# The state products of the decode streams as pairs in two halves of the array's rows, one pair behind each half of the output projection

## The chip, the cores and the metric

The kernel runs on one core of one Trainium2 chip. The metric is device time in microseconds (us) of one execution. The core has a matrix engine (TensorE; PE in the profile, PEld for its weight loads), a vector engine (VectorE, DVE), a scalar engine (ScalarE, ACT), a general engine (GpSimd, POOL) and a queue that issues most DMAs (SyncE, SP). All engines run side by side and wait for each other by semaphores; each one carries out its own instructions in order.

## The reference

One inference step of a two-layer trunk, on 1024 prompt frames and on 8 running streams of 16 frames each. Layer 0 is a gated MLP. Layer 1 is an mLSTM block with 4 heads of width 512; the change lies in it. For each head `h` and each running stream `b` the layer keeps a 512x512 matrix memory `C`:

```python
num   = einsum('bhts,bhse->bhte', s, v) + w_inter[..., None] * einsum('bhtd,bhde->bhte', q, C)
C_new = decay[..., None, None] * C + einsum('bhs,bhsd,bhse->bhde', w, k, v)
out   = (h + skip * xc) * silu(z);   y = x + out @ w_out
```

So for each of the 32 pairs of head and stream the 1 MB of old memory (`C0`) is read, multiplied by 16 query rows (the inter term of `num`), decayed, added to a product of 16 keys and 16 values, and written out (`C_sample`).

## The kernel before

Everything is single precision. A product that must be exact to about 24 bits is split in a high and a low part, and three matmuls are added up (high by high, high by low, low by high), each at the speed of one pass (type F32R).

**Streams.** Each pair of head and stream is one `Stream` (L1119). `load` (L1124) requests `sk48` (48 rows: the 16 keys and 16 values in the three combinations of high and low part, from the scratch tensor `st_d`) and the old memory as two tiles `c0` of 128x2x512 (256 of its 512 rows each). `products` (L1132) does two things. First the query product: 4 matmuls, one for each 128 rows of the memory, each using 32 of the array's 128 columns, so that the four lie side by side (`sm<-c,qT` in the profile; each is two instructions, so 8 rows of the trace). Its result is copied by ScalarE (`ev`, L1141). Then the state products: 4 matmuls of 48 rows by 128x512 (`sm<-sk`), each into a PSUM tile of its own; VectorE decays and adds each one into `c0` (L1148) and each half of `c0` is stored (L1150). Every fourth stream `finish` (L1152) gathers the query products (`sm<-ev,selm`).

**When streams run.** 10 of the 32 streams run inside the projection of `z` (a dense row of matmuls `sm<-xh,w` and `sm<-xl,w`, L867 to L879), placed by the table `plan` (L1433 to L1446). The other 22 run in the loop over units, one in each of the units 0 to 21 (L1490). The pools hold one `sk48` and four `c0` tiles (two streams).

**Units.** A unit is one 128-frame chunk of one head; there are 4 x 8. Unit n = 0 of a head is short, since it has no earlier state and no state update. In the order of TensorE, a unit does its own numerators (`sm<-va,s`, `sm<-Ch,q`), the state update (`sm<-va,k`), the scores of the next unit (`sm<-qT,kT`, `sm<-ident,kT`), the output projection of the unit two before (`project(prev2, 0)` and `(prev2, 1)`: 12 matmuls `sm<-w,o` each, for the two halves of the 1024 output columns; each half is added to `x1` by VectorE, L1399), the transposes of the unit before (`gate_pe`, `sm<-ident,hn`), and then the stream of this unit. The gate of the unit before follows those transposes: VectorE (`raw`, L1380), then GpSimd or, for chunks 0 to 2, VectorE (L1382), then ScalarE and GpSimd split the result into `o2` (`o<-raw`, L89 and L90), which the output projection of the next unit reads.

**What sets the order.** TensorE's order is the program's order. On the other engines a scheduler places each instruction by its own estimate of when its inputs are ready; there each engine is bound to the order that was written. PSUM has 8 tiles, all named `sm`, in rotation.

Of the kernel before, what the change touches and what calls it, by code (L numbers as in the profile page):

```python
# [8 lines left out]
F32 = mybir.dt.float32  # L9
F32R = mybir.dt.float32r  # L10
# [5 lines left out]
P = 128  # L16
# [54 lines left out]
def trunk_kernel(ctx: ExitStack, tc: tile.TileContext, ins: dict, outs: list):  # L71
# [12 lines left out]
    def f32(ap):  # L84
        return ap.bitcast(F32)
# [371 lines left out]
    def part(ks, q):  # L457
        return Xh[:, ks, quarter(q)], Xl[:, ks, quarter(q)]
# [660 lines left out]
    class Stream:  # L1119
# [2 lines left out]
            self.c0 = [None, None]  # L1122

        def load(self):  # L1124
            d, b = self.d, self.b
            self.sk = dw.tile([3 * SL, 2, DH], F32R, name="sk48")
            S.dma_start(out=f32(self.sk), in_=f32(st_d[d.h])[b])
            for hf in range(2):
                c0 = self.c0[hf] = dw.tile([P, 2, DH], F32, name="c0", bufs=4)
                S.dma_start(out=c0, in_=C0[b, d.h, hf * 256:(hf + 1) * 256].rearrange("(c p) e -> p c e", p=P))  # L1130

        def products(self):  # L1132
            d, b = self.d, self.b
            pa = ps.tile([P, DH], F32, name="sm")

            b2 = slice(b // 2 * 32, b // 2 * 32 + 32)
            for c in range(DC):
                T.matmul(pa[32 * c:32 * c + 32], d.g["qT"][:, c, b2], self.c0[c // 2][:, c % 2], start=True, stop=True)
            ev = dw.tile([P, DH], F32, name="ev", bufs=4)
            d.ev.append(ev)  # L1140
            d.last = A.copy(out=ev, in_=pa)  # L1141
            for hf in range(2):
                c0 = self.c0[hf]
                for cc in range(2):
                    c = hf * 2 + cc
                    pc = ps.tile([P, DH], F32, name="sm")
                    T.matmul(pc, self.sk[:, 0, c * P:(c + 1) * P], self.sk[:, 1, :], start=True, stop=True)
                    V.scalar_tensor_tensor(out=c0[:, cc], in0=c0[:, cc], scalar=decB[:, d.h, 8 + b:9 + b], in1=pc,  # L1148
                                           op0=ALU.mult, op1=ALU.add)
                S.dma_start(out=C_s[0, b, d.h, hf * 256:(hf + 1) * 256].rearrange("(c p) e -> p c e", p=P), in_=c0)  # L1150
# [16 lines left out]
    def open_head():  # L1167
        heads.append(Dec(len(heads), streams[-1].d.last if streams else None))

    def open_stream():  # L1170
        st = Stream(heads[len(streams) // SB], len(streams) % SB)
        streams.append(st)
        st.load()


    ld = ctx.enter_context(tc.tile_pool(name="ld", bufs=2, reuse_waits="tile"))
# [260 lines left out]
    for j in range(ZDEC):  # L1437
        k = first + int(j * rate)
        plan.setdefault(k, []).append(open_stream)
        plan.setdefault(k + 2, []).insert(0, lambda j=j: streams[j].products())  # L1440
        plan.setdefault(k + 3, []).insert(0, lambda j=j: streams[j].finish())
        if j % SB == SB - 3 and k + 3 <= 3 * NF:
            plan.setdefault(k, []).append(open_head)
            plan.setdefault(k + 1, []).append(lambda: heads[-1].queries())
            plan.setdefault(k + 2, []).append(lambda: heads[-1].keys())
            plan.setdefault(k + 3, []).append(lambda: heads[-1].normaliser())  # L1446
# [2 lines left out]

    def open_streams(i):  # L1450
        for _ in range(stream_at.count(i)):
            open_stream()
        return streams[len(streams) - stream_at.count(i):]

    def first_loads():
# [34 lines left out]
    for i, u in enumerate(units):  # L1490
# [44 lines left out]
                S.dma_start(out=x1[v.n], in_=x1_d[v.n])  # L1535
        if i + 1 < NU:
            project(prev2, 0)
            project(prev2, 1)
        gate_pe(prev)
        gate(prev)  # L1540
        gate2(prev)
# [7 lines left out]
        if rid3:  # L1549
            project(rid3, 0)  # L1550
            project(rid3, 1)
        for st in sts:
            st.products()
        next_streams = open_streams(i + 1)
        if rid2:
            gate_pe(rid2)
            gate(rid2)
# [49 lines left out]
```

## Time and profile before

| | |
|---|---|
| time, 3 runs | 1933.91 us median (1932.88 to 1936.3) |
| the profiled execution | 1929.5 us, span of its instructions 1927.8 us |
| granted TensorE clock | 0.996 of 2.4 GHz |
| TensorE busy | 1887.7 us (98%) |
| VectorE, ScalarE, GpSimd busy | 63%, 45%, 35% |
| DMA | 328.20 MB, 170 GB/s over the span |

The z projection with its 10 streams lies between about 1200 and 1385 us, the loop of units from there to the end. Busy times of TensorE are modelled ends; the distance from the start of one group to the start of the next is the safer measure.

### The profile page before, as it was taken

Reading aid. Unit: us, or ns where it says so; the run is one execution under the profiler, and the core shown is the slowest. Engines: PE = TensorE matmul, PEld = TensorE weight load, DVE = VectorE, ACT = ScalarE, POOL = GpSimd, SP = SyncE. Lnnn points to the kernel's source line nnn. Section 1 sums busy time; section 2 is a strip of 40 time slices with the busy share of each in tenths; the row PEclk is TensorE's granted clock in tenths of the full one; section 3 lists DMA queues with packets and bytes.
Section 4 is the critical chain, followed back from the end, with each engine's and each line's share of the span. In section 5 each row is a group of like instructions: output and inputs, shape, how many; then the busy total and the mean of one; then the engine's idle time right before and its main releaser. Section 6 shows DMA issues by size and latency. Waiting matters only on the chain.

```text
span 1927.8 us, 32016 instructions
## 1 busy us (share of the span) xinstructions
PE 1887.7 (98%) x11553; PEld 1676.0 (87%) x11553; DVE 1216.1 (63%) x2406; ACT 862.4 (45%) x1760; POOL 674.9 (35%) x725
## 2 busy tenths in 40 slices
PE   7999999999999999999999999999999999999998
PEld 6888999999999778888999989888977887788887
DVE  5832567777776454567666655222388687688786
ACT  5422444444444343446655554222354444444564
POOL 2000234444442000024444421100167457457586
PEclk9999999999999999999999999999999999999999
DMA  6222343333334854435555564787898898876543
GB/s 217 93 93 73 96 109 100 100 98 99 101 97 122 263 152 143 131 92 157 152 160 166 164 186 124 240 256 247 263 320 267 263 287 273 262 239 196 153 130 125
DMA packets 345305, 328.20 MB, mean 170 GB/s; under 512 B 28164, under 2 KB 276436, under 8 KB 345148
## 3 DMA queue, kind: packets, MB, share of 16 engines
q1 hardware_dynamic: 278444, 255.72, 43.4%
q10 hardware_dynamic: 66512, 69.85, 11.7%
q8 instruction: 91, 1.49, 0.3%
q14 instruction: 66, 0.54, 0.1%
q0 software_dynamic: 192, 0.59, 0.1%
HBM read 203.07 MB, written 123.02 MB: 169 GB/s over the span
## 4 chain that ended last, share of the span: by engine, by line
PE 79%; DMA 7%; DVE 5%; POOL 3%; ACT 2%; issue 2%; ACTq 0%; SPq 0%; POOLq 0%; DVEq 0%
PE sm L58 79%; DMA cw<-cw_d 1%; POOL Cl L90 1%; DMA out<-c 1%; DMA z_d<-st 1%; DVE c L1148 1%; POOL va L90 1%; DMA kT<-k_d 1%; DMA vv<-vb_d 1%; DMA c<-in_state_mlstm_C 1%; DVE raw L1380 0%; DVE w L90 0%; DMA st_d<-w 0%; POOL q L90 0%; DVE Cst L1297 0%
## 5 line engine op out<-in xcount | busy, mean ns | idle before, releaser
L58 PE MATMUL sm<-xh,w 128*128 128x384 f32 x1536 | 410.4, 341 | 1.8 <-issue 1.2
L58 PEld LDWEIGHTS sm<-xh,w 128*128 128x128 f32 x1536 | 281.0, 188 | 10.0 <-issue 6.5
L58 PE MATMUL sm<-xl,w 128*128 128x384 f32 x768 | 260.1, 339 | 0.0
L58 PE MATMUL sm<-Xh,w 128*128 128x288 f32 x1024 | 216.9, 299 | 4.3 <-ACT c L499 4.3
L58 PE MATMUL sm<-w,o 128*128 128x512 f32 x864 | 209.7, 398 | 2.1 <-ACT o L89 1.2
L58 PE MATMUL sm<-w,os 128*128 128x512 f32 x864 | 200.3, 393 | 4.5 <-ACT os L89 3.5
L58 PEld LDWEIGHTS sm<-w,os 128*128 128x128 f32 x864 | 162.4, 189 | 40.8 <-ACT os L89 6.0
L58 PEld LDWEIGHTS sm<-w,o 128*128 128x128 f32 x864 | 160.0, 188 | 40.2 <-ACT o L89 1.4
L58 PE MATMUL sm<-w,Xh 128*128 128x512 f32 x576 | 180.5, 394 | 0.9 <-DVE w L90 0.9
L58 PEld LDWEIGHTS sm<-Xh,w 128*128 128x128 f32 x1024 | 168.9, 190 | 4.7 <-ACT c L499 4.5
L58 PE MATMUL sm<-S,w 128*128 128x288 f32 x1152 | 163.8, 297 | 0.0
L90 DVE TENSOR_TENSOR w<-r,w 128x512 fp32r<-128x512 f32 x176 | 137.9, 790 | 35.1 <-ACT w L89 34.4
L58 PEld LDWEIGHTS sm<-S,w 128*128 128x128 f32 x1152 | 155.1, 188 | 0.8
L90 POOL TENSOR_TENSOR Cl<-Cst,Ch 128x514 fp32r<-128x514 f32 x96 | 128.7, 1352 | 73.6 <-ACT Ch L89 50.3
L58 PE MATMUL sm<-Xl,w 128*128 128x288 f32 x512 | 151.9, 297 | 0.0
L58 PEld LDWEIGHTS sm<-xl,w 128*128 128x128 f32 x768 | 144.8, 189 | 0.0
L90 DVE TENSOR_TENSOR w<-raw,w 128x1024 fp32r<-128x1024 f32 x43 | 55.9, 1300 | 130.6 <-ACT w L89 126.6
L89 ACT CAST w<-r 128x512 fp32r<-128x512 f32 x176 | 107.2, 618 | 61.5 <-PE sm L58 29.1
L58 PEld LDWEIGHTS sm<-w,Xh 128*128 128x128 f32 x576 | 108.2, 190 | 24.0 <-DVE w L90 1.8
L58 PE MATMUL sm<-w,Xl 128*128 128x512 f32 x288 | 113.0, 392 | 0.0
L90 DVE TENSOR_TENSOR os<-or,os 128x384 fp32r<-128x384 f32 x96 | 52.8, 555 | 88.0 <-ACT os L89 87.8
L58 PE MATMUL sm<-va,k 128*128 128x258 f32 (+1 forms) x768 | 102.9, 284 | 0.5 <-DVE raw L1380 0.4
(310 smaller groups left out, 3643.5 us busy)
## 6 DMA issues: line engine op xcount, KB each, us to landing
c<-in_state_mlstm_C SPq DMA_DIRECT2D x64, 512.0 KB
out<-c SPq DMA_DIRECT2D x64, 512.0 KB
r<-in_a_w_in SPq DMA_DIRECT2D x96, 256.0 KB
or<-o_d SPq DMA_DIRECT2D x96, 192.0 KB
raw<-in_b_w_in SPq DMA_DIRECT2D x32, 512.0 KB
qT<-q_d SPq DMA_DIRECT2D x40, 256.0 KB
vh<-v_d SPq DMA_DIRECT2D x48, 192.0 KB
vb_d<-st ACTq DMA_DIRECT2D x48, 192.0 KB
```

Source lines behind the costliest of these rows:

```text
L58: ins = fn(*args, **kw)
L89: first = A.copy(out=hi, in_=src)
L90: (lo_eng or V).tensor_tensor(out=lo, in0=src, in1=f32(hi), op=ALU.subtract)
L1148: V.scalar_tensor_tensor(out=c0[:, cc], in0=c0[:, cc], scalar=decB[:, d.h, 8 + b:9 + b], in1=pc, op0=ALU.mult, op1=ALU.add)
```

## The change

The 4 state products of a stream become 2 pairs. `sk48` is held twice, on partitions 0 to 47 and 64 to 111 (two requests instead of one, so 192 KB more for each stream), and the two matmuls of a pair take one copy each, so that they use different halves of the array's rows. `products` now ends after the first pair (`part(0)`); the second is `part(1)`. In the units the query product and the first pair stand between the two halves of the output projection, the second pair behind the second half, and the transposes of the unit before come after that. The `C0` of the next stream is requested between the pairs, its `sk48` behind the second pair. Inside the z projection both pairs stand together, where the four matmuls stood.

```diff
         def load(self):
+            self.load_c0()
+            self.load_sk()
+
+        def load_sk(self):
             d, b = self.d, self.b
-            self.sk = dw.tile([3 * SL, 2, DH], F32R, name="sk48")
-            S.dma_start(out=f32(self.sk), in_=f32(st_d[d.h])[b])
+
+            self.sk = dw.tile([64 + 3 * SL, 2, DH], F32R, name="sk48")
+            for r0 in (0, 64):
+                S.dma_start(out=f32(self.sk)[r0:r0 + 3 * SL], in_=f32(st_d[d.h])[b])
+
+        def load_c0(self):
...
             d.last = A.copy(out=ev, in_=pa)
-            for hf in range(2):
+            self.part(0)
+
+        def part(self, hf):
...
                 c0 = self.c0[hf]
-                for cc in range(2):
+                pcs = [ps.tile([P, DH], F32, name="sm") for _ in range(2)]
+                for cc, pc in enumerate(pcs):
                     c = hf * 2 + cc
-                    pc = ps.tile([P, DH], F32, name="sm")
-                    T.matmul(pc, self.sk[:, 0, c * P:(c + 1) * P], self.sk[:, 1, :], start=True, stop=True)
+                    rs = slice(64 * cc, 64 * cc + 3 * SL)
+                    T.matmul(pc, self.sk[rs, 0, c * P:(c + 1) * P], self.sk[rs, 1, :], start=True, stop=True)
+                for cc, pc in enumerate(pcs):
                     V.scalar_tensor_tensor(out=c0[:, cc], in0=c0[:, cc], scalar=decB[:, d.h, 8 + b:9 + b], in1=pc,
                                            op0=ALU.mult, op1=ALU.add)
...
-        plan.setdefault(k + 2, []).insert(0, lambda j=j: streams[j].products())
+        plan.setdefault(k + 2, []).insert(0, lambda j=j: (streams[j].products(), streams[j].part(1)))
...
         if i + 1 < NU:
             project(prev2, 0)
+        for st in sts:
+            st.products()
+        next_streams = open_streams(i + 1)
+        if i + 1 < NU:
             project(prev2, 1)
+        for st in sts:
+            st.part(1)
+        for st in next_streams:
+            st.load_sk()
         gate_pe(prev)
         gate(prev)
         gate2(prev)
...
-        for st in sts:
-            st.products()
-        next_streams = open_streams(i + 1)
```

On TensorE, at the end of unit 8, the first unit of head 1, before (`w,o` is the output projection, `c` and `sk` the stream's two kinds of product, `ident,hn` the transposes for the gate):

```order
L58 MATMUL sm<-w,o_15667 128x512 x24
L58 MATMUL sm<-ident,hn 128x128 x4
L58 MATMUL sm<-c_15693,qT 32x512 x2
L58 MATMUL sm<-c_15695,qT 32x512 x2
L58 MATMUL sm<-sk_15691 128x512 x4
L58 MATMUL sm<-va_12485,s_15745 128x258 x3
```

and the same place now:

```order
L58 MATMUL sm<-w,o_15713 128x512 x12
L58 MATMUL sm<-c_15674,qT 32x512 x2
L58 MATMUL sm<-c_15676,qT 32x512 x2
L58 MATMUL sm<-sk_15699 128x512 x2
L58 MATMUL sm<-w,o_15713 128x512 x12
L58 MATMUL sm<-sk_15699 128x512 x2
L58 MATMUL sm<-ident,hn 128x128 x4
L58 MATMUL sm<-va_12485,s_15764 128x258 x3
```

The stream's products moved ahead of the transposes, and these now stand directly before the next unit's numerators.

On VectorE, from the end of unit 7 into unit 8, before (`x1` is the addition of a projected half, `raw` the gate's four instructions, `c0` the four state additions, `dd` the masking of the scores that were computed in unit 8):

```order
L1399 TENSOR_TENSOR x1_5_14031<-x1_5_14031,sm_15628 128x512
L1399 TENSOR_TENSOR x1_5_14031<-x1_5_14031,sm_15642 128x512
L1380 SCALAR_TENSOR_TENSOR raw_15661<-sm_15656,colB_235,sk_15492 128x128 x4
L1148 SCALAR_TENSOR_TENSOR c0_15488<-c0_15488,decB_12439,sm_15677 128x512
L1148 SCALAR_TENSOR_TENSOR c0_15488<-c0_15488,decB_12439,sm_15680 128x512
L1148 SCALAR_TENSOR_TENSOR c0_15490<-c0_15490,decB_12439,sm_15684 128x512
L1148 SCALAR_TENSOR_TENSOR c0_15490<-c0_15490,decB_12439,sm_15687 128x512
```

and now:

```order
L1415 TENSOR_TENSOR x1_5_14042<-x1_5_14042,sm_15646 128x512
L1164 SCALAR_TENSOR_TENSOR c0_15440<-c0_15440,decB_12439,sm_15667 128x512
L1164 SCALAR_TENSOR_TENSOR c0_15440<-c0_15440,decB_12439,sm_15668 128x512
L1415 TENSOR_TENSOR x1_5_14042<-x1_5_14042,sm_15678 128x512
L1164 SCALAR_TENSOR_TENSOR c0_15442<-c0_15442,decB_12439,sm_15692 128x512
L1164 SCALAR_TENSOR_TENSOR c0_15442<-c0_15442,decB_12439,sm_15693 128x512
L1396 SCALAR_TENSOR_TENSOR raw_15707<-sm_15702,colB_235,sk_15510 128x128 x4
```

Two state additions moved ahead of the second projected half, and the gate stands behind all four instead of ahead of them.

On ScalarE in unit 8, before (`o` is the high part of the gated rows that the next output projection reads, `s` the high part of the masked scores):

```order
L1329 COPY hn<-sm 128x256
L89 CAST o_15667<-raw 128x512
L1241 ACTIVATE k_15741<-sm,tok 128x512
L89 CAST s_15745<-dd 128x128
L89 CAST q_15750<-dd 128x128
```

and now:

```order
L1345 COPY hn<-sm 128x256
L1257 ACTIVATE k_15760<-sm,tok 128x512
L89 CAST s_15764<-dd 128x128
L89 CAST o_15713<-raw 128x512
L89 CAST q_15769<-dd 128x128
```

The split of `o` moved behind that of `s`. It is the same in unit 16.

## Rows read from the trace of the kernel before

**Rows 1.** The page: TensorE's busy share, and the chain that ended last.
```profile
PE 1887.7 (98%) x11553; PEld 1676.0 (87%) x11553; DVE 1216.1 (63%) x2406; ACT 862.4 (45%) x1760; POOL 674.9 (35%) x725
...
PE 79%; DMA 7%; DVE 5%; POOL 3%; ACT 2%; issue 2%; ACTq 0%; SPq 0%; POOLq 0%; DVEq 0%
```

**Rows 2.** Busy time by stage, 1372 to 1780 us.
```profile
1372.00:1780.00 408.00, 402.36 (x2654) 329.31 (x2653) 315.17 (x679) 186.56 (x368) 235.67 (x213) 1.00 0.85 264
```

**Rows 3.** Groups by shape from 1200 us: busy us, mean ns, idle before.
```profile
L58 PE MATMUL sm<-sk 48*128 48x512 f32 x128 | 39.3, 422 | 4.2 <-DVE x L1399 3.4 <-DMA sk<-st_d 0.8
...
L58 PE MATMUL sm<-c,qT 128*32 128x512 f32 x256 | 34.1, 605 | 0.0
```

**Rows 4.** Timeline at a stream, loads too: start, us, xcount.
```profile
1498.61 0.16 PEld L58 LDWEIGHTS sm<-c,qT 128*32 128x32 f32 x8 [0.37 <-issue]
1498.62 1.06 PE L58 MATMUL sm<-c,qT 128*32 128x512 f32 x8
```

**Rows 5.** Timeline, TensorE, a stream inside the z projection.
```profile
1251.23 1.06 PE L58 MATMUL sm<-c,qT 128*32 128x512 f32 x8
1252.23 1.19 PE L58 MATMUL sm<-sk 48*128 48x512 f32 x4
1253.35 0.45 PE L58 MATMUL sm<-xh,w 128*128 128x384 f32 x1
```

**Rows 6.** Timeline, TensorE, output projection directly before C0.
```profile
1492.85 5.84 PE L58 MATMUL sm<-w,o 128*128 128x512 f32 x24
```

**Rows 7.** Timeline, all engines, end of unit 7, start of unit 8.
```profile
1509.03 5.83 PE L58 MATMUL sm<-w,o 128*128 128x512 f32 x24
...
1514.70 0.60 PE L58 MATMUL sm<-ident,hn 128*128 128x128 f32 x4
1514.90 0.69 DVE L1399 TENSOR_TENSOR x<-x,sm 128x512 f32<-128x512 f32 x1 [2.11 <-PE sm L58]
...
1515.23 1.07 PE L58 MATMUL sm<-c,qT 128*32 128x512 f32 x8
1515.50 1.12 DVE L1380 SCALAR_TENSOR_TENSOR raw<-sm,colB,sk 128x128 f32<-128x128 f32 x4
...
1516.22 1.17 PE L58 MATMUL sm<-sk 48*128 48x512 f32 x4
...
1516.75 2.72 DVE L1148 SCALAR_TENSOR_TENSOR c<-c,decB,sm 128x512 f32<-128x512 f32 x4
...
1517.32 0.98 PE L58 MATMUL sm<-va,s 128*128 128x258 f32 x6
...
1518.61 0.62 ACT L89 CAST o<-raw 128x512 fp32r<-128x512 f32 x1
...
1520.28 5.83 PE L58 MATMUL sm<-w,o 128*128 128x512 f32 x24
```

**Rows 8.** Timeline, TensorE, a stream with a transpose behind it.
```profile
1750.73 2.71 PE L58 MATMUL sm<-w,o 128*128 128x512 f32 x11
1753.28 0.60 PE L58 MATMUL sm<-ident,hn 128*128 128x128 f32 x4
...
1754.80 1.31 PE L58 MATMUL sm<-sk 48*128 48x512 f32 x4
1756.04 0.66 PE L58 MATMUL sm<-ident,hn 128*128 128x128 f32 x4
```

**Rows 9.** Timeline, all engines, unit 24, which has no stream.
```profile
1790.53 0.60 PE L58 MATMUL sm<-ident,hn 128*128 128x128 f32 x4
...
1790.89 0.97 PE L58 MATMUL sm<-va,s 128*128 128x258 f32 x6
1791.34 1.12 DVE L1380 SCALAR_TENSOR_TENSOR raw<-sm,colB,sk 128x128 f32<-128x128 f32 x4
...
1794.59 0.61 ACT L89 CAST o<-raw 128x512 fp32r<-128x512 f32 x1
...
1795.25 2.14 PE L58 MATMUL sm<-w,o 128*128 128x512 f32 x8 [1.17 <-ACT o L89]
```

More of the change, by code (lines that the diff above doesn't have):

```diff
@@ L1124, in load @@
         def load(self):
+            self.load_c0()
+            self.load_sk()
+        def load_sk(self):
             d, b = self.d, self.b
-            self.sk = dw.tile([3 * SL, 2, DH], F32R, name="sk48")
-            S.dma_start(out=f32(self.sk), in_=f32(st_d[d.h])[b])
+            self.sk = dw.tile([64 + 3 * SL, 2, DH], F32R, name="sk48")
+            for r0 in (0, 64):
+                S.dma_start(out=f32(self.sk)[r0:r0 + 3 * SL], in_=f32(st_d[d.h])[b])
+        def load_c0(self):
+            d, b = self.d, self.b
             for hf in range(2):
@@ L1141, in products @@
             d.last = A.copy(out=ev, in_=pa)
-            for hf in range(2):
+            self.part(0)
+        def part(self, hf):
+            d, b = self.d, self.b
+            if True:
                 c0 = self.c0[hf]
-                for cc in range(2):
+                pcs = [ps.tile([P, DH], F32, name="sm") for _ in range(2)]
+                for cc, pc in enumerate(pcs):
                     c = hf * 2 + cc
-                    pc = ps.tile([P, DH], F32, name="sm")
-                    T.matmul(pc, self.sk[:, 0, c * P:(c + 1) * P], self.sk[:, 1, :], start=True, stop=True)
+                    rs = slice(64 * cc, 64 * cc + 3 * SL)
+                    T.matmul(pc, self.sk[rs, 0, c * P:(c + 1) * P], self.sk[rs, 1, :], start=True, stop=True)
+                for cc, pc in enumerate(pcs):
                     V.scalar_tensor_tensor(out=c0[:, cc], in0=c0[:, cc], scalar=decB[:, d.h, 8 + b:9 + b], in1=pc,
@@ L1168, in open_head, with open_stream @@
         heads.append(Dec(len(heads), streams[-1].d.last if streams else None))
-    def open_stream():
+    def open_stream(whole=True):
         st = Stream(heads[len(streams) // SB], len(streams) % SB)
         streams.append(st)
-        st.load()
+        (st.load if whole else st.load_c0)()
     ld = ctx.enter_context(tc.tile_pool(name="ld", bufs=2, reuse_waits="tile"))
@@ L1451, in open_streams @@
         for _ in range(stream_at.count(i)):
-            open_stream()
+            open_stream(i == 0)
         return streams[len(streams) - stream_at.count(i):]
```

## The prediction

> **What bounds the kernel now.** I read the page's busy shares first: TensorE is busy 98% of the span, and the chain that ended last runs through it for 79% [rows 1]. So what counts is TensorE's own time, and after it the few waits in which it stands still. Then the groups by shape, for the work that the change touches: 128 state products (`sk`) and 256 instructions of the query product (`c,qT`); before the former TensorE idled 4.2 us in all, 3.4 of them until VectorE had added a projected half and 0.8 until the first `sk48` had landed [rows 3]. Then the timelines, where the distance between two starts gives the price of a group in its place. The reader is to see three prices there.
>
> - One matmul of 512 columns in a dense row: 11 of the output projection take 1753.28 - 1750.73 = 2.55 us, 0.232 us each [rows 8].
> - Four state products take 1253.35 - 1252.23 = 1.12 us inside the z projection [rows 5], where 4 x 0.232 = 0.93 would do. The other 0.19 us is the price of being a block of another form (48 of 128 rows) between blocks of other forms. A part of it falls at the way out: 24 matmuls of the projection with `c` behind them take 1498.62 - 1492.85 = 5.77 us [rows 4, 6], with the transposes behind them 5.67 us [rows 7], so 0.10 us; the rest, 0.09 us, at the way in. I take 0.20 us for each change of form, both parts together.
> - Different columns of the array do work at the same time: the eight instructions of a query product take 0.605 us each, but all are over in 1.06 us [rows 3, 4], and their eight weight loads start within 0.16 us [rows 4].
>
> **The pair itself** does not occur in the trace, as no two matmuls there use different rows. The bounds: as close as the query products in different columns, then a pair costs one matmul, 0.232 us; or one after the other, as now, 0.464 us. Below one matmul it cannot go, as 512 columns have to pass. I take the near end, since row halves share still less than column groups do. The Trainium skill (TensorE: Matmul & The Clock Gate, Part 3, measured speedup) has 3.07 times for four row groups of 32 instead of 4; by that, an estimate, each further matmul in parallel would cost about 0.1 of one, and 64 pairs 1.5 us more than in my sum. No run here shows it yet.
>
> **The change part by part.** I count on TensorE from block to block.
>
> 1. *Streams in the z projection, 10 of them.* The changes of form stay three (into `c`, into `sk`, out), and four matmuls become two slots: -2 x 0.232 = -0.46 us each, **-4.6 us** (0 if the pairs don't overlap). Nothing else waits there: TensorE is dense.
> 2. *Units 0 and 1* have no projection yet, so both pairs stand together: -0.46 in unit 0. In unit 1 the transposes come directly behind a pair. Four state products with transposes behind take 1756.04 - 1754.80 = 1.24 us [rows 8], with numerators behind 1.10 us [rows 7], so 0.14 us more, and some 0.1 us again for the way on. Together **-0.7 us**.
> 3. *Units 2 to 21.* Two slots are saved (-0.46), but five changes of form stand where three stood: into `c`, into the first pair, out to the second half of the projection, into the second pair, out to the transposes: +0.40. The transposes directly behind a pair cost the 0.14 us of point 2, and the change from the transposes into `c`, which cost 1515.23 - 1514.70 = 0.53 us [rows 7] for a group that takes 0.36 us in unit 24 (1790.89 - 1790.53) [rows 9], goes with the move. That comes out between -0.06 and +0.07; I take 0.03 in 18 units, and 0.1 in units 9 and 17, where the gathering of four streams now has a change of form more. **+0.7 us** (-1.2 to +1.4 for all 20). So in the units the pairs pay only for their own coming and going.
> 4. *The gate comes later, and in units 8 and 16 TensorE will wait for it.* Before, the transposes start at 1514.70, 2.62 us ahead of unit 8's numerators (1517.32); VectorE does the gate at 1515.50, ahead of the four state additions, ScalarE splits `o` at 1518.61, and the projection starts at 1520.28, 2.96 us behind the numerators, without a wait [rows 7]. Now the transposes start 0.4 us ahead of the numerators, and the gate stands behind two more state additions. The trace has the like of it in unit 24, which has no stream: transposes directly ahead of the numerators, gate at 1791.34, `o` split at 1794.59, and the projection at 1795.25, 4.36 us behind the numerators, after 1.17 us of idle time [rows 9]. Now in unit 8: the second half's addition starts 0.2 us behind the projection's end [rows 7], some 0.85 us before the numerators; it and two state additions (0.6 + 2 x 0.68, from 2.72 us for four) put the gate at 1.1 us behind the numerators' start, where unit 24 has 0.45. ScalarE's order now has `o` behind `s` as in unit 24, so the same chain ends 0.65 us later than there: 5.0 us, against 2.96 now. That is 2.0 us in each of two units, **+4.0 us** (0, if the chain has slack that I don't see, to 5). Longer units have the slack: in unit 7 the projection starts at 1509.03 [rows 7], some 8.3 us behind its numerators (the query product ahead of them starts at 1498.62 [rows 4] and it and the state products take 2.1 us).
> 5. *Waits that go.* The 3.4 us before state products [rows 3] come where VectorE is held by an earlier wait and the fourth product finds no free PSUM tile. With the products spread over the projection, two of the four tiles are freed early, and VectorE's being held costs TensorE nothing until the next unit's numerators need a tile. **-2.5 us** (0 to -3.4). What is late next then are the state additions and the gate behind them, under the next unit's numerators and updates.
> 6. *The second copy of `sk48`.* 32 x 192 KB = 6.3 MB more over DMA engines that are busy 0.85 in the units [rows 2]. Behind the request on SP stand the stores of `c0` and the loads of the next units, as before; the request waits for the second pair, which ends about where the fourth product ended, and even in unit 8 it has some 7 us until the next first pair (2.96 us to the projection, 12 x 0.232 for its half, 1.0 for the query product, and more with the wait of point 4). Only the first stream, which waits 0.8 us for its copy already [rows 3], will wait for the second one: **+0.5 us** (0 to 1.5). The earlier request of `C0` is worth nothing: TensorE has no wait for `C0` now (idle 0.0 before `c,qT` [rows 3]).
>
> The sum: -4.6 - 0.7 + 0.7 + 4.0 - 2.5 + 0.5 = -2.6 us. Against the profiled execution (1929.5 us, 1.7 more than its span) that is 1926.9 us. The three timed runs have their median 4.4 us above the profiled one, at 1933.91, so on their scale I forecast **1931.3 us**. What a measurement can tell from no change is 0.2%, 3.9 us; the forecast lies within it.
>
> **The rivals.**
>
> - *The gate's lateness costs nothing* (point 4 falls away, for instance since `o` is ready before `s` after all): -6.6 us, 1927.3. For it: GpSimd and ScalarE have idle time in unit 8. Against it: unit 24 shows the wait with an easier start. 0.25.
> - *The row halves take turns* (slower). Then each of 64 pairs costs 0.232 us more, 14.8 us, and the changes of form remain as pure cost: 1931.3 + 14.8 = 1946.1. For it: nothing in the trace shows rows in parallel. Against it: columns are. It decides from a distance of about 0.1 us between the two starts of a pair; at 0.232 it is this case. 0.12.
> - *Only the weight loads take turns*: a load of 128 columns in a new form delays its matmul by about 0.09 to 0.1 us, and a pair that enters a new form would pay it twice. There are 10 + 2 + 40 = 52 such pairs: +5 us, 1936.3. Against it: eight loads for different columns within 0.16 us. 0.08.
> - *The fuller DMA engines make other loads late*, above all `cw`, which VectorE waits for ahead of the second addition: about what the old waits cost twice over, +6 us, 1937. 0.10.
> - My own sum, 1928 to 1934 around 1931.3: 0.45.
>
> **How the numbers follow.** Faster by over 0.2% (below 1930.0): most of the first rival, 0.21, and a quarter of my own case, 0.11: 0.32. Slower by over 0.2% (above 1937.8): the turns, 0.12, and 0.08 from the upper sides of the others: 0.20. The rest, 0.48, is within. The range leaves out the row halves' turns at the top and the best tenth at the bottom: 1925.5 to 1940.
>
> **What would show each step.** In the z projection the distance from the first state product to the next `xh` should fall from 1.12 to about 0.66 us, with the two starts of a pair within 0.02 us. In a middle unit, from the projection's first half to the next numerators TensorE should need the same time as before within 0.1 us. In units 8 and 16 a wait for `o` of about 2 us should stand before the projection, and the 3.4 us of waits before `sk` should be gone or under 1 us. The first pair should wait 1 to 2 us for its second copy. The forecast is wrong if the starts of a pair lie 0.1 us or more apart, or if no wait stands in units 8 and 16.

## The result

The changed kernel takes **1940.21 us** (median of 11 runs, 1935.59 to 1945.47) against 1930.87 us of the kernel before (11 runs, 1923.11 to 1936.3): the ratio is 1.0054, 95% interval 1.0038 to 1.0070. It is half a per cent slower. The forecast was 1931.3 us (1925.5 to 1940), no measurable change. The profiled execution is the slowest of the 11 (1945.47 us, span 1943.6), so its waits are on the large side; where sizes matter below, medians decide.

The page has TensorE almost as busy as before [rows 1], for 0.8 us less:

```profile
PE 1886.9 (97%) x11553; PEld 1666.6 (86%) x11553; DVE 1215.5 (63%) x2406; ACT 863.5 (44%) x1760; POOL 680.1 (35%) x725
```

From 1372 to 1780 us TensorE was busy for 390.7 us of 408 (402.4 in [rows 2]), and the DMA share rose from 0.85 to 0.89:

```profile
1372.00:1780.00 408.00, 390.68 (x2589) 312.58 (x2588) 305.81 (x663) 182.55 (x359) 226.53 (x202) 0.99 0.89 272
```

**The pairs work.** The groups by shape from 1200 us (answering [rows 3]): the 128 state products, whose mean is 479 ns, cover 29.5 us; 128 x 479 ns are 61.3, so two run at a time. By the trace's start times the two of a pair begin 3 to 4 ns apart in 58 of the 64 pairs; only in the first stream, which waits for its copies, are they clearly apart (1.38 and 0.31 us). In the z projection (answering [rows 5]) the block of four goes from 1.12 to 0.67 us, two slots of 0.232 and the 0.20 for a change of form:

```profile
L58 PE MATMUL sm<-c,qT 128*32 128x512 f32 x256 | 34.1, 605 | 0.0
L58 PE MATMUL sm<-sk 48*128 48x512 f32 x128 | 29.5, 479 | 3.6 <-DMA sk<-st_d 2.7 <-DVE c L1164 0.9
```
```profile
1270.22 1.07 PE L58 MATMUL sm<-c,qT 128*32 128x512 f32 x8
1271.21 0.73 PE L58 MATMUL sm<-sk 48*128 48x512 f32 x4
1271.88 0.44 PE L58 MATMUL sm<-xh,w 128*128 128x384 f32 x1
```

**The gate is late, as forecast.** The timeline at the start of unit 8 (answering [rows 7]). The gate's first operation stands 1.18 us behind the numerators (forecast 1.1), the projection 5.10 us (forecast 5.0), after 1.90 us of idle time; in unit 16 it is 1.91 us:

```profile
1524.42 0.50 PE L58 MATMUL sm<-sk 48*128 48x512 f32 x2
1524.85 0.66 PE L58 MATMUL sm<-ident,hn 128*128 128x128 f32 x4
1525.13 1.40 DVE L1164 SCALAR_TENSOR_TENSOR c<-c,decB,sm 128x512 f32<-128x512 f32 x2
1525.27 0.98 PE L58 MATMUL sm<-va,s 128*128 128x258 f32 x6
...
1526.45 1.12 DVE L1396 SCALAR_TENSOR_TENSOR raw<-sm,colB,sk 128x128 f32<-128x128 f32 x4
...
1529.70 0.61 ACT L89 CAST o<-raw 128x512 fp32r<-128x512 f32 x1
1530.37 4.60 PE L58 MATMUL sm<-w,o 128*128 128x512 f32 x12 [1.90 <-ACT o L89]
```

**And there are waits that I had not forecast.** TensorE's waits from 1200 to 1800 us (us in total, times, longest) add up to 21.1 us. Of the kernel before the same view adds up to 7.3 us; its 3.6 us for `x` are gone.

```profile
PE sm L58 <- DVE Cst L1313: 4.6, 6, 1.5
PE sm L58 <- ACT o L89: 3.8, 2, 1.9
PE sm L58 <- ACT q L89: 3.7, 1, 3.7
PE sm L58 <- DMA sk<-st_d: 2.7, 1, 2.7
PE sm L58 <- DVE w L90: 2.3, 2, 1.1
PE sm L58 <- ACT hn L1345: 1.2, 2, 0.8
PE sm L58 <- ACT ev L1150: 1.0, 2, 0.6
PE sm L58 <- DVE k L1258: 0.9, 1, 0.9
PE sm L58 <- DVE c L1164: 0.9, 1, 0.9
```

Where they fall is read by comparing the start of the numerators of the same unit in both traces:

| point | before | after | later by | on the way there |
|---|---|---|---|---|
| unit 0 | 1385.64 | 1387.91 | 2.3 | first stream waits 3.6 us |
| unit 2 | 1405.08 | 1412.72 | 7.6 | waits for `k` and `q`, 4.6 us, in unit 1 |
| unit 7 | 1500.73 | 1505.11 | 4.4 | old waits gone, 1.5 us of them for `x` |
| unit 9 | 1528.58 | 1540.15 | 11.6 | 7: `Cst`, 2.0 us; 8: `o`, 1.9 us |
| unit 15 | 1640.25 | 1652.84 | 12.6 | 10: `hn`, `Cst`, `w`, 2.3 us |
| unit 19 | 1702.60 | 1721.20 | 18.6 | 15, 16 and 18, as 7, 8 and 10 |
| unit 24 | 1790.89 | 1805.51 | 14.6 | an old wait of 1.7 us gone |
| end | 1927.8 | 1943.6 | 15.8 | |

The waits in units 7, 10, 15 and 18 begin on SP. In unit 7 the two requests of the next head's output weights left 8.9 us ahead of the numerators in the kernel before, ahead of the request of `sk48`:

```profile
1491.80 0.90 SPq L144 DMA_DIRECT2D raw<-in_b_w_out  x2
...
1500.83 0.32 SPq L1127 DMA_DIRECT2D sk<-st_d  x1
```

Now they leave 3.2 us ahead of them, behind the first half's store and both requests of `sk48`, which wait for VectorE and for the second pair. ScalarE then waits 5.8 us for the first weight, VectorE's split stands ahead of the state updates `Cst`, and TensorE waits for these (by the names, for a free PSUM tile):

```profile
1499.35 0.38 SPq L1166 DMA_DIRECT2D out<-c  x1
1499.82 2.04 SPq L1133 DMA_DIRECT2D sk<-st_d  x2
1501.91 0.90 SPq L144 DMA_DIRECT2D raw<-in_b_w_out  x2
```
```profile
1507.86 1.05 ACT L89 CAST w<-raw 128x1024 fp32r<-128x1024 f32 x1 [5.75 <-DMA raw<-in_b_w_out]
```
```profile
1510.41 2.05 DVE L90 TENSOR_TENSOR w<-raw,w 128x1024 fp32r<-128x1024 f32 x1 [4.41 <-ACT w L89]
```
```profile
1512.91 0.63 PE L58 MATMUL sm<-va,k 128*128 128x256 f32 x3 [1.52 <-DVE Cst L1313]
```

In unit 1 it is, by the profile, a store of the z projection that ScalarE waits for: the last one left at 1391.43, and `q` was written only at 1397.58:

```profile
1391.43 0.33 ACTq L878 DMA_DIRECT2D z_d<-st  x1
...
1397.58 0.30 ACT L89 CAST q<-dd 128x128 fp32r<-128x128 f32 x1 [3.87 <-DMA z_d<-st]
```

**Some waits cost more than they last.** Columns as in [rows 2]; the third from the end is the granted clock. Behind four of the waits TensorE ran at 0.50, 1.2 GHz instead of 2.4, for 3.41 us by the trace, 1.71 us lost each time, 6.8 in all; behind the 1.91 us of unit 16 it did not:

```profile
1231.00:1234.00 3.00, 3.00 (x10) 2.79 (x10) 1.99 (x3) 0.00 (x0) 0.00 (x0) 0.50 0.60 152
1235.00:1238.00 3.00, 3.00 (x19) 3.00 (x18) 0.00 (x0) 0.49 (x1) 0.00 (x0) 1.00 0.93 290
1398.20:1401.40 3.20, 3.20 (x15) 2.98 (x15) 0.88 (x4) 2.02 (x4) 0.82 (x2) 0.50 1.11 363
1514.20:1517.40 3.20, 3.20 (x14) 3.10 (x15) 2.97 (x11) 0.40 (x1) 1.62 (x2) 0.50 0.62 217
1531.30:1534.50 3.20, 3.20 (x9) 2.51 (x8) 0.16 (x1) 0.82 (x1) 1.42 (x3) 0.50 1.14 330
1675.00:1680.00 5.00, 4.46 (x23) 2.59 (x23) 1.80 (x7) 2.37 (x5) 2.80 (x4) 1.00 1.07 340
```

So for this execution: TensorE's idle time, summed over the whole trace, rose from 32.7 to 49.3 us (+16.6), the clock took 6.8, and what is left of the 15.8 us, its own work, fell by 7.6 (15.8 - 16.6 - 6.8). TensorE did get faster; the waits and the clock took back more than that.

### The profile page after: what moved, and what is told of

Same layout as the page of the kernel before. It is cut to its first block, busy times and chain, and to the rows that moved or that the text cites. A ratio compares the mean times of both kernels' runs of the same rounds, so it can differ in the third digit from the quotient of the medians.

```text
span 1943.6 us, 32061 instructions
## 1 busy us (share of the span) xinstructions
PE 1886.9 (97%) x11553; PEld 1666.6 (86%) x11553; DVE 1215.5 (63%) x2406; ACT 863.5 (44%) x1760; POOL 680.1 (35%) x725
## 4 chain that ended last, share of the span: by engine, by line
PE 78%; DMA 9%; DVE 6%; ACT 3%; issue 2%; POOL 2%; SPq 1%; ACTq 0%; POOLq 0%; DVEq 0%
PE sm L58 78%; DMA raw<-in_b_w_out 2%; DMA z_d<-st 1%; DMA st_d<-w 1%; DVE w L90 1%; DMA r<-in_a_w_in 1%; ACT w L89 1%; DMA raw<-in_b_w_in 1%; DMA out<-c 1%; DMA vh<-v_d 1%; POOL Cl L90 1%; DVE Cst L1313 1%; DVE c L1164 1%; DMA sk<-st_d 1%; DVE raw L1396 0%
## 5 line engine op out<-in xcount | busy, mean ns | idle before, releaser
L58 PE MATMUL sm<-w,o 128*128 128x512 f32 x864 | 217.7, 403 | 9.5 <-ACT o L89 5.0
L90 POOL TENSOR_TENSOR Cl<-Cst,Ch 128x514 fp32r<-128x514 f32 x96 | 132.6, 1395 | 82.5 <-ACT Ch L89 74.8
```

What stands on the lines that cost most here:

```text
L58: ins = fn(*args, **kw)
L90: (lo_eng or V).tensor_tensor(out=lo, in0=src, in1=f32(hi), op=ALU.subtract)
```

## The experiments

Each run is shown by the main lines of what differs; the sentence above them says what else does. Two theories at first. *Order*: the new place is to blame, through late weights and the late gate. *Volume*: 6.3 MB more on the DMA engines are. All medians below stand beside 1929 to 1932 us for the kernel before, run on the same chip each time; ratios have 95% intervals.

**1. The two halves of the change, and the copies alone.**

Pairs in the old place, with the requests in the old order (`sk48`, then `C0`):
```diff
             project(prev2, 0)
-        for st in sts:
-            st.products()
-        next_streams = open_streams(i + 1)
-        if i + 1 < NU:
             project(prev2, 1)
-        for st in sts:
-            st.part(1)
-        for st in next_streams:
-            st.load_sk()
...
             project(rid3, 1)
+        for st in sts:
+            st.products()
+            st.part(1)
+        next_streams = open_streams(i + 1)
```


> The pairs and the second copy of sk48 as in the changed kernel, but both pairs of a stream in the old place (behind the transposes and whole projection), and the requests in the old order (sk48, then C0). Order theory (the loss comes from the place: on SP the loads of the output weights now stand behind the request of sk48 and the store ahead of it, so VectorE splits the weights late; and the gate is late in units 8 and 16): no such waits, a pair for two matmuls saves 0.46 us in each of 32 streams, -14.7 us, less 1 to 4 us for the first stream's copy: about 1918 us (1915 to 1921), with no wait of 1 us or more for Cst, w or o in units 7 to 18. Volume theory (6.3 MB more on full DMA engines make all other loads late): the waits of units 0/1, 7, 9 and 15 to 18 stay, 10 to 14 us of them, and eat the saving: 1927 to 1935 us.

1932.00 us, 1.0007 (0.9992 to 1.0022): the volume theory's number, though not all of its waits. Those for late weights are gone, as the order theory says, but 3.7 us for `q` in unit 1 stay and others are new (4.0 us for `raw`, 3.2 for `ev`), so nothing is gained.

The move alone:
```diff
-            self.sk = dw.tile([64 + 3 * SL, 2, DH], F32R, name="sk48")
-            for r0 in (0, 64):
+            self.sk = dw.tile([3 * SL, 2, DH], F32R, name="sk48")
+            for r0 in (0,):
...
-                    rs = slice(64 * cc, 64 * cc + 3 * SL)
+                    rs = slice(0, 3 * SL)
```


> The move without the pairs: two products behind each half of the projection and C0 requested between, but all four from one copy of sk48 in the same 48 rows. Order theory: the waits for Cst and w in units 7, 9, 15 and 17 (8 us in the profiled execution of the changed kernel) and for o in units 8 and 16 (3.8 us) are here too, and the new changes of form are not paid for by pairs: 20 x 0.5 us more on TensorE, -3 us of old waits: +15 to +22 us, about 1949 us. Volume theory: without the second copy the waits for Cst and w are under 1 us in all: +8 to +12 us, about 1941 us. Either way the first stream waits 0.8 us or so for its copy, and units 0 and 1 have no wait of 3.7 us, if that wait comes from the copies' bytes.

1940.51 us, 1.0048 (1.0029 to 1.0067): as slow as with the pairs, and the volume theory's number. The waits for `o` are there (1.7 us each), those for `w` are not, and unit 1 waits 0.5 us instead of 3.7. The weights do leave late here too, behind the one request of `sk48`, 5.6 us ahead of unit 7's numerators at 1508.29 (8.9 before, 3.2 in the changed kernel), and TensorE doesn't wait for them. Between these runs the place makes 3.3 us of the delay, and the second request the other 2.4:

```profile
1502.69 0.89 SPq L144 DMA_DIRECT2D raw<-in_b_w_out  x2
```

The second copy alone:
```diff
-            S.dma_start(out=f32(self.sk), in_=f32(st_d[d.h])[b])
+            for r0 in (0, 64):
+                S.dma_start(out=f32(self.sk)[r0:r0 + 3 * SL], in_=f32(st_d[d.h])[b])
```


> The kernel before, with sk48 loaded twice as in the changed kernel; the products read the first copy alone, four one after the other in the old place, and the second copy is read by nothing. It shows the price of the copies by itself. Order theory: the same as before within 0.2% (1929 to 1935 us), with some 1 to 3 us at the first stream. Volume theory: 6 to 12 us slower (1937 to 1943), with waits for loads (w, cw, raw, st) in the units and at the step from unit 0 to 1.

1934.43 us, 1.0019 (1.0008 to 1.0030): a price of 2.8 us, below what the volume theory needs by itself. By my own sum the pairs should bring -14.7 us in the old place. With the copies it is +0.4 against the kernel before; against the copies alone, the pairs bring 2.4.

In the profiled execution of pairs in the old place, where TensorE is early in the z projection, one place shows how they are eaten. ScalarE waits 8.4 us for a weight of the projection, the copy of `ev` stands behind it in its queue, and TensorE waits 2.7 us:

```profile
1334.75 1.04 ACT L89 CAST w<-raw 128x1024 fp32r<-128x1024 f32 x1 [8.40 <-DMA raw<-in_b_w_in]
1335.70 0.48 ACT L877 ACTIVATE st<-sm 128x384 f32<-128x384 f32 x1
1336.08 0.58 ACT L1150 COPY ev<-sm 128x512 f32<-128x512 f32 x1
```
```profile
1336.71 1.44 PE L58 MATMUL sm<-ev,selm 128*32 128x512 f32 x2 [2.71 <-ACT ev L1150]
```

**2. One wait at a time.** The weights requested ahead of `sk48` (their splits stay in place):
```diff
+        if u.n == 6 and u.h + 1 < H:
+            raws[u.h + 1] = [fetch_w(b_wo[4 * u.h + 4 + k]) for k in (0, 1)]
+        if prev and prev.n == 0 and prev.h:
+            raws[prev.h] = [fetch_w(b_wo[4 * prev.h + k], state["last"]) for k in (2, 3)]
         for st in next_streams:
             st.load_sk()
```


> The changed kernel, with one thing else: the two requests of the next head's output weights in units 7, 9, 15, 17 (and 23, 25) are issued ahead of the request of sk48 on SP, as they are in the kernel before; the splits stay in place. Order theory: the waits for Cst and for w in units 7, 9/10, 15 and 17/18 (2.0, 2.3, 1.1 and 2.6 us in the profiled execution) fall under 0.5 us each, and with them the stretch at the lower clock behind the first: 7 to 10 us less than the changed kernel, about 1932 us; the waits for o in units 8 and 16 stay at 1.9 us. Volume theory: the weights are late by the traffic, not by their place; no more than 2 us less than the changed kernel, 1938 to 1942 us.

1942.93 us, 1.0067 (1.0048 to 1.0086). The waits for `Cst` and `w` are gone, as the order theory says, and the time is not. GpSimd now splits a weight ahead of `o`, and units 6 and 14 wait 2.0 us for that:

```profile
PE sm L58 <- POOL o L90: 3.9, 2, 2.0
PE sm L58 <- ACT o L89: 3.8, 2, 1.9
PE sm L58 <- ACT q L89: 3.3, 1, 3.3
PE sm L58 <- ACT ev L1150: 2.7, 1, 2.7
```

The gate ahead of the second pair:
```diff
             project(prev2, 1)
+        gate_pe(prev)
+        gate(prev)
+        gate2(prev)
         for st in sts:
             st.part(1)
         for st in next_streams:
             st.load_sk()
-        gate_pe(prev)
-        gate(prev)
-        gate2(prev)
```


> The changed kernel, with the transposes and the gate of the unit before put back ahead of the second pair (behind the whole projection and the first pair), so that VectorE does the gate ahead of two state additions and ScalarE splits o earlier. My account of the change: the waits for o in units 8 and 16 (1.9 us each, seen in every kernel with the moved products) fall under 0.5 us, and with them up to 1.7 us each at the lower clock: 4 to 7 us less than the changed kernel, 1934 to 1937 us. Rival (the engines' queues are so tight that a wait taken away turns up at another place, as when the weights went first): no more than 2 us less, 1939 to 1943 us.

1941.25 us, 1.0057 (1.0043 to 1.0070). The waits for `o` fall to 0.39 us each, those for `w` grow to 3.1 us, and 1.9 us for `raw` are new. Again the wait moved, as the rival had it.

**3. With room on the DMA engines,** and pairs only where they seemed to pay. Three kernels leave out one line, the store of `C_s`:
```diff
-                S.dma_start(out=C_s[0, b, d.h, hf * 256:(hf + 1) * 256].rearrange("(c p) e -> p c e", p=P), in_=c0)
```


> The kernel before, leaving out the 64 stores of the new states C_s (512 KB each, 33.6 MB of the 153 MB that the DMA engines move between 1200 and 1790 us), so that these engines have room: the base for the next two. Both theories: the waits for late loads go, 3 to 8 us less than before, about 1926 us; its idle time of TensorE between 1200 and 1780 us is under 4 us.

> Pairs and second copy with both pairs in the old place and the old order of requests, leaving out the stores of C_s. Traffic theory (the pairs do save 0.46 us in each of 32 streams, but where the streams run the loads arrive only just in time, so that a faster TensorE waits for them instead, and the copies' 6.3 MB make it worse): with room on the DMA engines 12 to 15 us less than the kernel before without stores. Rival, another engine or the clock takes the gain (VectorE's or ScalarE's order, the lower clock behind each wait): 0 to 5 us less, as with the stores.

> The changed kernel, leaving out the stores of C_s. What remains against the kernel before without stores is the price of the place, without late loads: -4.6 us in the z projection, 0 to +2 us for the changes of form in the units, two waits for o of 1.9 us each, with up to 1.7 us each for a stretch at the lower clock. Traffic theory: between -2 and +3 us of the base, and no wait of 1 us or more for Cst, w or q. Rival (the order of requests on SP makes the loads late whatever the traffic): the waits of units 7, 9, 15 and 17 stay, +6 to +10 us.

1922.26, 1918.99 and 1935.31 us. Fewer bytes help the kernel before by 8.6 us: it too pays for its traffic. Pairs then bring 3.3 us, not 12 to 15, the rival's number. The changed kernel stands 13.1 above its base, more than either expectation, and 16.3 above the pairs in the old place, with `o` at 1.9 us twice, `w` at 1.4 and 1.3 and `hn` at 2.6, though the DMA share from 1372 to 1780 us is 0.74 (0.89 with the stores). So the place has a price of its own.

Pairs in the units alone, both in the old place:
```diff
-            for r0 in (0, 64):
+            for r0 in (0, 64)[:1 + self.two]:
```


> Pairs in the old place for the 22 streams of the units alone; the ten streams in the z projection keep one copy and four products one after the other. Traffic theory: in the z projection, where pairs in the old place lost 4 us instead of saving 4.6, nothing is lost now, and the units save 22 x 0.46 = 10.1 us less the copies (2.8 us for all 32, so 1.9 us) and less what new waits at the change of head eat (5 us in the profiled execution of the kernel with pairs everywhere): 1925 to 1929 us. Rival (what TensorE saves anywhere comes back as waits in full): the same as before, 1930 to 1934 us.

1930.09 us, 0.9995 (0.9976 to 1.0014): the rival's number.

**4. Is it VectorE's queue?** Without the state additions:
```diff
-                    V.scalar_tensor_tensor(out=c0[:, cc], in0=c0[:, cc], scalar=decB[:, d.h, 8 + b:9 + b], in1=pc,
-                                           op0=ALU.mult, op1=ALU.add)
```


> The kernel before, leaving out the 128 state additions on VectorE (0.68 us each, 2.7 us in each of 32 streams), so that C0 is stored as it was loaded; the products run and nobody reads them. All transfers stay as they are. The base for the next. VectorE theory (its queue is what TensorE runs into): 4 to 8 us less than before. Loads theory: 0 to 3 us less, since the waits of VectorE for cw, sk and zz stay.

> Pairs and second copy in the old place, leaving out the 128 state additions on VectorE. VectorE theory: with 2.7 us less on VectorE in each unit the pairs' 14.7 us come through, 11 to 14 us less than the kernel before without additions. Loads theory (what TensorE saves it waits for loads, directly or through an engine that is held by one): 0 to 5 us less than that base.

1933.68 and 1936.09 us, 1.0021 (1.0009 to 1.0034) and 1.0028 (1.0014 to 1.0041). Taking 87 us of work from VectorE gains nothing, and pairs gain nothing on top. So it is unlikely that VectorE is simply too busy. But the loads theory's numbers are missed too, and so is its reason: VectorE's waits for loads between 1372 and 1780 us don't stay, they fall from 21.0 to 6.7 us (`cw` most of all; first line before, second without additions), while TensorE itself now waits 5.8 us for a load of `qT`. What holds the gain back here is open:

```profile
DVE dd L1230 <- DMA cw<-cw_d: 16.5, 6, 4.6
DVE dd L1228 <- DMA cw<-cw_d: 4.1, 5, 1.5
PE sm L58 <- DMA qT<-q_d: 6.3, 2, 5.8
```

**5. Smaller copies.** Rows in DRAM become keys 0, 1, values, keys 2, 3; each half of the array's rows loads only its 768 columns. A pair is columns c and c+2 (the slices and the additions follow), it stands in the old place, and both halves of `C0` are stored behind the second pair:
```diff
-            self.sk = dw.tile([64 + 3 * SL, 2, DH], F32R, name="sk48")
-            for r0 in (0, 64):
-                S.dma_start(out=f32(self.sk)[r0:r0 + 3 * SL], in_=f32(st_d[d.h])[b])
+            self.sk = dw.tile([64 + 3 * SL, 768], F32R, name="sk48")
+            for cc in range(2):
+                S.dma_start(out=f32(self.sk)[64 * cc:64 * cc + 3 * SL], in_=f32(st_d[d.h])[b, :, 256 * cc:256 * cc + 768])
...
+                    if hf:
+                        S.dma_start(out=C_s[0, b, d.h, cc * 256:(cc + 1) * 256].rearrange("(c p) e -> p c e", p=P), in_=c0)
```


> Pairs in the old place, with smaller copies: each half of the rows gets only the keys that its two products need (147 KB for each copy instead of 192), so that a stream loads 295 KB instead of 384, half as much more than the 192 KB of the kernel before; a pair is then columns c and c+2 of the state, and both halves of C0 are stored behind the second pair. Traffic theory: half of what the copies cost comes back, 1.5 to 4 us less than the kernel with full copies (1932.0), 1928 to 1930.5 us. Rival (bytes don't matter at this size): the same, 1931 to 1934 us.

1924.11 us, 0.9970 (0.9956 to 0.9985): faster than both kernels, and by more than expected. It differs from the pairs of 1 in the bytes and in the late stores. With the late stores and full copies:
```diff
-                S.dma_start(out=f32(self.sk)[64 * cc:64 * cc + 3 * SL], in_=f32(st_d[d.h])[b, :, 256 * cc:256 * cc + 768])
+                S.dma_start(out=f32(self.sk)[64 * cc:64 * cc + 3 * SL], in_=f32(st_d[d.h])[b])
```


> As the kernel with three-quarter copies (pairs of columns c and c+2 in the old place, both halves of C0 stored behind the second pair), but each half of the rows gets the full 192 KB again, 384 KB for a stream instead of 295. Bytes theory: back to the first kernel with pairs, 1930 to 1934 us. Stores theory (storing both halves together, behind the second pair, is what helped): 1922 to 1926 us.

1930.29 us, 1.0001 (0.9987 to 1.0015). It is the bytes: 6 us for 89 KB in each of 32 streams. The late stores change little in this place (1932.0 with early ones).

The same edit for smaller copies, made in the changed kernel instead of in the old place:

> The changed kernel's places and order of requests, with the three-quarter copies and the pairing c and c+2. If the place costs what it did without pairs (9 us: the waits for o, the late weights and two more changes of form in each unit), 8 to 11 us more than in the old place, 1932 to 1935 us. If place and bytes have one cause (loads that arrive too late), the place costs less now that there are fewer bytes, 1925 to 1930 us. The waits for o in units 8 and 16 (1.9 us each) should be there in both cases.

1943.85 us, 1.0065 (1.0043 to 1.0087), slower than both expectations. The waits of the z projection and of unit 1 are gone (0.5 and 0.7 us are left), but the units are worse, `w` above all:

```profile
PE sm L58 <- DVE w L90: 6.9, 2, 3.5
PE sm L58 <- ACT o L89: 3.8, 2, 1.9
```

**6. All together.** The changed kernel with both edits of 2 and the smaller copies of 5:

> The changed kernel's places, with three-quarter copies (pairs c and c+2), the output weights requested ahead of sk48, and the gate ahead of the second pair. If the list of costs is complete (late weights, late gate, changes of form), only the changes of form are left: the kernel with small copies in the old place (1924.1) plus 20 x 0.49 us, 1932 to 1936 us, with no wait for w, Cst or o above 0.6 us in units 7 to 18. If the waits only change their place (a split of w on GpSimd or VectorE ahead of o, as when the weights alone went first): 1938 to 1944 us. If the changes of form are hidden after all: 1924 to 1929 us.

**1922.30 us, 0.9950 (0.9935 to 0.9966)**, the lowest median of the kernels that leave nothing out. It is below every expectation, but its interval overlaps that of the small copies in the old place (0.9956 to 0.9985), so a gain by the move itself is not shown. The changes of form are not hidden: from the projection's first half to the next numerators a middle unit takes 8.25 us here and 7.87 in the kernel of 5 with small copies (from the starts in both traces), 0.38 us more. TensorE's waits from 1200 to 1800 us add up to 7.3 us here and 9.2 there; the largest:

```profile
PE sm L58 <- ACT o L89: 2.0, 3, 1.2
PE sm L58 <- DVE Cst L1319: 1.8, 2, 1.1
PE sm L58 <- ACT q L89: 1.7, 1, 1.7
PE sm L58 <- DMA sk<-st_d: 1.1, 1, 1.1
```

Three more runs take things back from it. Without the smaller copies, their pairing and their late stores, so that both edits of 2 alone are left:

> The changed kernel with both orders mended (output weights requested ahead of sk48, gate ahead of the second pair) and its full copies. If the loss is the order, and the two waits hide each other (so that each alone mended nothing): 1926 to 1931 us, some 10 to 14 less than the changed kernel, and the waits for w, Cst and o in units 7 to 18 fall from 11.9 us to under 4. If the bytes were the larger part: 1934 to 1939 us.

1943.54 us, 1.0069 (1.0045 to 1.0093), slower than both expectations: both orders mended, the changed kernel's copies and stores. Unit 8 waits 0.39 us for `o`, `w` not at all; the waits of the z projection and unit 1 are back.

With full copies and nothing else changed (the edit of the second diff in 5):

> The best kernel so far (new places, both orders mended, pairs c and c+2, both halves of C0 stored behind the second pair) with one thing changed: each half of the rows gets the full 192 KB, 384 KB for a stream instead of 295. Bytes theory (as in the old place, where full copies cost 6.2 us against small ones): 1930 us or more, up to 1943. Stores theory (the early store of the first half, between the requests, is what costs the time in the new place): 1922 to 1927 us.

1933.01 us, 1.0006 (0.9991 to 1.0021). Full copies alone cost 10.7 us here, the early store of the first half (and the pairing, which changed with it) another 10.5. In the profiled execution it is the wait for `ev` in the z projection, 4.2 us, that is back (0.3 with small copies):

```profile
PE sm L58 <- ACT ev L1150: 4.2, 1, 4.2
```

And both edits of 2 without pairs, all products from one copy (the edit of the move alone in 1):

> The same order without pairs: one copy of sk48, four products one after the other, two behind each half. If the pairs' 14.8 us on TensorE come through where the waits are out of the way: 14 us more than with pairs and small copies (1922.3), 1934 to 1938 us. If waits take most of it again: 1925 to 1930 us, and then the gain over the kernel before comes from the order and not from the pairs.

1936.90 us, 1.0038 (1.0020 to 1.0055). Against the kernels before of the same runs the mended order without pairs is 6.1 us slower, with pairs and small copies 6.8 faster, 12.9 us between them. That is the size of what the pairs save on TensorE (14.8 us), but the two kernels differ in the stores as well: without pairs the first half is still stored early. A run without pairs and with late stores is missing, so the pairs' own share of the 12.9 is not shown.

The runs with pairs side by side (medians, us):

| | full copies, early stores | full copies, late stores | small copies, late stores |
|---|---|---|---|
| old place | 1932.0 | 1930.3 | 1924.1 |
| new place, orders of the changed kernel | 1940.2 | not run | 1943.9 |
| new place, both orders mended | 1943.5 | 1933.0 | 1922.3 |

The pairing c and c+2 comes with the late stores. In the new place the two orders are worth some 21 us with small copies and late stores, and nothing with the full copies and early stores of the changed kernel.

## Why the prediction was wrong

Its steps one by one; the points in brackets are the prediction's.

1. *Bounds of the pair, streams in the z projection* (point 1): right on TensorE (0.67 us a block). The estimate that I made from the 3.07 of the Trainium skill (TensorE: Matmul & The Clock Gate, Part 3, measured speedup), 1.5 us for 64 pairs, is not borne out: a block is two slots and one change of form. The span model of that section, about 4 ns for each further matmul, is what the trace shows (3 to 4 ns). The sentence that failed is "Nothing else waits there: TensorE is dense". Unit 0 came 2.3 us later, not 4.6 earlier.
2. *Units 0 and 1, and 2 to 21* (points 2 and 3): the groups take about what was worked out (a change of form 0.20, transposes behind a pair); pairs pay for their coming and going. A middle unit takes 8.24 us from the projection to the next numerators in place of 8.30, -0.06 where I took +0.03; the terms as written (-0.46 + 0.40 + 0.14 - 0.17) add up to -0.09, not to -0.06 to +0.07. That the place by itself is dear showed in the move alone, +9 us, for which these terms without the pairs' saving (0.03 + 0.46 us in 20 units), the gate (+4.0) and the old waits (-2.5) give 11.3.
3. *The gate in units 8 and 16* (point 4): right, 1.90 and 1.91 us against 2.0. Not in the sum: the lower clock behind the first.
4. *Waits that go* (point 5): right, the old 3.6 us for `x` are gone.
5. *The second copy of `sk48`* (point 6) is **the step that failed**, in its wait and in its price. "Behind the request on SP stand the stores of `c0` and the loads of the next units, as before": the output weights stood behind it too, and left 5.7 us later against the numerators (3.3 in the move alone). This could have been read from SP's order ahead of the run. And the price of +0.5 us: the first stream alone waits 3.6 us in place of 0.8, and against the move alone, which has one copy and no pairs, pairs and copies together bring 0.3 us (1940.2 and 1940.5), where the sum had some 14 (14.8 less 0.5). The full copies' extra bytes cost 6 us in the old place and 10.7 in the mended one (runs of 5 and 6); in the places looked at it is loads that came late for ScalarE, which holds what TensorE needs behind them in its queue.
6. *Clock:* 6.8 us in the profiled execution, for which the sum had no term. The mean of the granted clocks listed for the runs is 0.991 for the changed kernel and 0.993 for the one before, by my estimate some 4 us of 1940 (the difference of the means times the span). It is 0.990 for the small copies in the changed kernel and 0.989 for the mended orders with full copies, 6 and 7 of their 13 us by the same estimate, and 0.994 for both together: so a part of each loss is time at 1.2 GHz.

Of the rivals, the fuller DMA engines (0.10, 1937 us) came nearest to what happened, but named `cw`, and had only a part of the cause. What I can't show is how the loss divides: the terms don't add. With the orders mended alone, or with small copies and late stores alone, the kernel stays 13 us above the one before; with both it is 7 below. Late stores were never changed alone in the new place. Only one execution of each kernel is profiled, and runs of one kernel differ by up to 16 us. In the old place 7 us of the pairs' 14.7 stay unaccounted for even with small copies (in the profiled executions 4: from the first stream to the end it takes 692.4 us, 703.2 before). With full copies neither room on the DMA engines (3) nor on VectorE (4) brought the saving out.

## What to carry to other kernels

Here a TensorE that is 98% busy was still paced in part by the traffic beside it (8.6 us less without the stores, 6 to 11 for smaller copies), and what it saved became waits. So cost a change by the queues behind it, not by TensorE's slots alone. When a request moves, list everything that stands behind it in its queue, from the order of the changed kernel. And when mending one wait moves the time to another, mend them together before judging: here, in the new place, the two orders, and smaller copies with late stores, were each worth nothing, and together 0.9% of the changed kernel's time (1922.3 against 1940.2). And keep the old place in the comparison: smaller copies with late stores took 7.9 us off the kernel with pairs there, with no change of order (1924.1 against 1932.0), and whether the new place is better at all is not shown.

## What had not been expected of the hardware

- Two matmuls of 48 rows in rows 0 to 47 and 64 to 111, for different PSUM tiles, overlap in full: starts 3 to 4 ns apart, four products in 0.67 us where one after the other they took 1.12.
- In the changed kernel's trace four places with 1.9 to 4.6 us of waits were each followed by 3.41 us at 1.2 GHz, 1.71 us more, and a fifth was not, after the same wait (1.90 us in unit 8: yes; 1.91 in unit 16: no).
